# One hybrid decoder layer: half of the first FFN matrix by seven block products, the second matrix over eight banks, a longer gate queue and another first norm

## The chip, the core and the metric

The kernel runs on one core of one Trainium2 chip. The metric is the device time in microseconds of one execution. The profile shows one execution; its span is the time from the first to the last instruction.

## What is computed

One layer on 512 tokens of width 1024, all in float32: a norm, one wide projection, three causal attention mixers (sparse top-k, compressed and windowed, dilated), gates for each mixer, an output projection, and a gated FFN of hidden width 2816. Cut to what matters here:

```python
h = _rms(x, norm1_g)
(a_q, a_k, a_v, i_q, i_k, i_w, b_q, b_kv, b_g, c_qkv, mix_g) = _split_last(h @ w_in, IN_SIZES)
...                                    # three attentions give y_a, y_b, y_c of width 1024
g = sigmoid(mix_g).reshape(bsz, seq, 3, D_MODEL)
x = x + (g[:, :, 0] * y_a + g[:, :, 1] * y_b + g[:, :, 2] * y_c) @ w_out
h = _rms(x, norm2_g)
gate, up = split(h @ w_ffn_in, 2)      # each 512 x 2816
x = x + (silu(gate) * up) @ w_ffn_out
```

## The kernel before

**Matmuls in three passes.** Every large matrix product is done on pairs: a tensor is split into a high part in fp32r and a low part, the rest (`split`, lines 81 and 82: ScalarE casts, VectorE or GpSimd subtracts). `mm3` (lines 106 to 108) then issues three matmuls for each contraction block of 128: high by high, high by low, low by high. `weights` loads a block of a matrix by DMA on SP's queue (`raw`, five buffers, line 93) and splits it (`whi`, `wlo`, six buffers each, two contraction blocks of 256 columns in each); it is issued with high priority, so it runs as far ahead as buffers allow. The order of instructions on each engine is laid down ahead of the run by the framework, by priority and by the free buffers.

**The front.** Four tiles of 128 tokens are loaded on SP's queue. For each, `norm_sums` takes the squares of one half on ScalarE (line 162) and of the other on VectorE (line 164), `norm_T` adds the two sums (line 170), GpSimd makes the reciprocal root (lines 149 and 151), VectorE and ScalarE scale a half each (`hn`, lines 176 and 178), TensorE transposes eight blocks (line 111), VectorE multiplies the gain in (`gx`, line 188), and the result is split into `xh` and `xl`, one low part on GpSimd and one on VectorE. The first projection ("narrow", 220 columns, tokens stationary) follows, then all others, 256 weight columns at a time.

**Gates and merges.** For each of three branches and eight blocks of 128 output features, `gate` projects (24 matmuls of 512 columns, `pm<-xh,whi` and its two companions) and puts a tanh into a `tz` buffer (line 962, three buffers). `merge` projects the branch's heads (`pm<-oT`), combines the two (line 979) and writes to or reads from a DRAM tile `dz` (lines 973 and 984). A queue `due` keeps one gate ahead of each merge. The attention's steps are advanced between the halves of these projections (`tick`).

**Output projection and second norm.** `w_out` is taken in four groups of 256 columns, tokens stationary (`pf<-whi,zh`). In the last group each token tile is normalised, transposed and split into `xh2`, `xl2`.

**FFN.** The first matrix is taken in eleven chunks of 256 gate and 256 up columns. In a chunk the weights stand still and the hidden columns move: 2 (gate, up) x 2 column halves x 8 contraction blocks x 3 passes = 96 matmuls of 512 tokens. Chunk 0 is done in two token halves of 256, 192 matmuls, since the second half's norm comes later. After each half chunk ScalarE takes a tanh (line 1127), VectorE two gating operations (lines 1128 and 1129), and the result is split at once into `hh`, `hl`. The second matrix runs over 22 contraction blocks twice, once for each 512 output columns, into four PSUM banks at a time; tokens are stationary (`pf<-whi,hh`). At the end of each pass the last three blocks are done bank by bank, and each bank is added to the residual and written out (lines 1150 and 1151).

Of the kernel before, what the change touches and what calls it, by code (L numbers as in the profile page):

```python
# [67 lines left out]
def block_kernel(ctx: ExitStack, tc: tile.TileContext, x, norm1_g, norm2_g, w_in, qk_norm_g, cmp_pos, cmp_w,  # L68
# [60 lines left out]
    ip = ipx.enter_context(tc.tile_pool(name="init", bufs=1))  # L129
    with tc.high_priority():  # L130
# [4 lines left out]
    gT = ip.tile([128, KC], F32, name="gT")  # L135
    nc.scalar.dma_start(gT, norm1_g[0].rearrange("(k p) -> p k", p=128))
# [30 lines left out]
    def norm_T(xt, t, ss, n, g, xh, xl, pst, tmp, lo):  # L167

        s1 = ty.tile([128, 16], F32, name="nss", tag="ss")
        nc.vector.tensor_reduce(out=s1[:, 0:1], in_=ss[:, 0:n], op=ALU.add, axis=AX.X)  # L170
        r = rstd(s1, 1, 1.0 / D)
        hn = tmp.tile([128, D], F32, name="hn", tag="hn", bufs=2)
        for q in range(2):
            hs = slice(q * 512, q * 512 + 512)
            if q == 0:
# [4 lines left out]
        for q in range(2):  # L180
# [4 lines left out]
            if g is not None:  # L185
                g3 = g[:, 4 * q:4 * q + 4].unsqueeze(2).to_broadcast([128, 4, 128])
                gx = tmp.tile([128, 4, 128], F32, name="gx", tag="gx", bufs=2)
# [20 lines left out]
    xl = xp.tile([128, KC, S], F32R, name="xl", tag="xl")  # L208
    for t in range(NT):
# [42 lines left out]
    def proj_tm(segs, evac, then=None):  # L252
        width = sum(n for _, n in segs)
        wk = weights(w_in, segs, list(range(KC)), pool=PP)
# [29 lines left out]
    def tmt(name):  # L284
        return ap_.tile([128, NT, 256], F32, name=name, tag="tm", bufs=3)
# [80 lines left out]
    def narrow():  # L366
# [25 lines left out]
        proj_tm([(C_AKV, 128), (C_IK, 68), (C_BG, 24)], evac, then=then)  # L392
# [157 lines left out]
    def causal_probs(q, i, k, tab, topk, gate):  # L550
# [4 lines left out]
        if topk is not None:  # L555
            tm_ = ab.tile([128, S], F32, name="tabm", tag="tabm", bufs=2)
# [394 lines left out]
    def gate(bi, f):  # L951
# [9 lines left out]
        tz = ap_.tile([128, 2, S], F32, name="tz", tag="tm", bufs=3)  # L961
# [96 lines left out]
    norms = []  # L1058
    for c in range(0, D, 256):
# [11 lines left out]
        for t in range(NT):  # L1071
# [10 lines left out]
            if last:  # L1082
                norms.append(norm_T(xg[t], t, ss2[t], 4, None, xh2, xl2,
                                    lambda: m2_tile().rearrange("p (k c) -> p k c", c=128), np_,
                                    (nc.vector, nc.vector)))
                next(norms[t])

# [18 lines left out]
    for j in range(2):  # L1106
        ffn_in(pus[j], wu, j, lo_t, 4, KC)
        ffn_in(pus[j], wu, j, hi_t)
    nx.close()
    zx.close()  # L1110

    hp_ = ctx.enter_context(tc.tile_pool(name="hid", bufs=1, reuse_waits="tile"))
    hh_, hl_ = [], []
    for c in range(0, DFF, 256):
        if c:
            wg = weights(w_fi, [(c, 256)], list(range(KC)))
            pgs = [m2_tile() for _ in range(2)]
            for j in range(2):
                ffn_in(pgs[j], wg, j)
            wu = weights(w_fi, [(DFF + c, 256)], list(range(KC)))  # L1120
            pus = [m2_tile() for _ in range(2)]
        for j in range(2):
            pu = pus[j]
            if c:
                ffn_in(pu, wu, j)
            th = hp_.tile([128, S], F32, name="fth", tag="fth", bufs=2)
            nc.scalar.activation(th, pgs[j], AF.Tanh, scale=0.5)
            nc.vector.scalar_tensor_tensor(out=th, in0=th, scalar=1.0, in1=pgs[j], op0=ALU.add, op1=ALU.mult)
            nc.vector.scalar_tensor_tensor(out=th, in0=th, scalar=0.5, in1=pu, op0=ALU.mult, op1=ALU.mult)
            f = c // 128 + j  # L1130
            a = hp_.tile([128, S], F32R, name=f"hh{f}")
            b = hp_.tile([128, S], F32R, name=f"hl{f}")
            split(a, b, th)
            hh_.append(a)
            hl_.append(b)
# [35 lines left out]
```

## Time and profile before

| | us |
|---|---|
| median of 3 runs | 993.58 |
| lowest, highest | 992.93, 999.28 |
| the profiled execution | 991.78 |
| its span | 990.0 |

In the span TensorE is busy 971.0 us, VectorE 564.9, ScalarE 436.5 and GpSimd 174.0. Busy time of TensorE is modelled, and overlapping matmuls hide their own latency in it; so the number of matmuls in a stretch says more than the busy share. The stretches: front to about 29 us, projections and attention to about 573, output projection to about 616, second norm and chunk 0 to 647, ten chunks to 863, second matrix to 986, output to 990.

### The profile page before, as it was taken

What the parts mean: (1) busy time and instruction counts of PE and PEld (TensorE: products, weight loads), DVE (VectorE), ACT (ScalarE), POOL (GpSimd) and SP (SyncE); (2) the same over time, 40 slices, a digit from 0 to 9 for tenths busy, and PEclk for the clock granted to TensorE, in tenths of its full rate; (3) what the DMA queues carried; (4) which work ended last, traced back from release to release, by engine and by line L of the source; (5) the groups of instructions that cost most, each with busy time, mean ns of one, the idle gap of its engine ahead of it and who ended that gap; (6) DMA issues with size and microseconds to landing.
All of it is one profiled execution on the core that took longest, in us unless ns stands there. A gap on an engine that the chain in (4) does not pass through costs nothing.

```text
span 990.0 us, 16079 instructions
## 1 busy us (share of the span) xinstructions
PE 971.0 (98%) x5887; PEld 823.7 (83%) x5887; DVE 564.9 (57%) x1277; ACT 436.5 (44%) x956; POOL 174.0 (18%) x156
## 2 busy tenths in 40 slices
PE   6999999999999899999999999999999999999998
PEld 5889999899887577777778899988888888888886
DVE  6699999766665666574764645454344344422321
ACT  5544555756565655564534434443333233322220
POOL 3234565543100221131110312000000000000000
PEclk9999999999999999999999999999999999999999
DMA  8541344433332244367613452233333333322421
GB/s 210 123 128 44 86 119 128 120 116 110 104 96 66 79 129 121 118 167 195 187 57 89 140 201 86 86 101 110 88 88 108 104 85 96 110 93 96 139 75 42
DMA packets 119264, 109.91 MB, mean 111 GB/s; under 512 B 19931, under 2 KB 105234, under 8 KB 119186
## 3 DMA queue, kind: packets, MB, share of 16 engines
q1 hardware_dynamic: 116994, 107.85, 37.6%
q10 hardware_dynamic: 2192, 1.05, 0.4%
q8 instruction: 46, 0.75, 0.3%
q14 instruction: 32, 0.26, 0.1%
HBM read 96.66 MB, written 12.21 MB: 110 GB/s over the span
## 4 chain that ended last, share of the span: by engine, by line
PE 93%; DMA 3%; DVE 2%; ACT 1%; issue 1%; SPq 1%; POOL 0%; DVEq 0%; ACTq 0%; POOLq 0%
PE pf L107 14%; PE pf L108 14%; PE pf L106 14%; PE pm L107 13%; PE pm L106 13%; PE pm L108 13%; PE tr L111 4%; PE ovb L541 2%; PE lg L364 2%; PE lg L363 2%; PE ova L541 1%; DMA c_in<-dC 1%; PE lg L849 1%; DMA raw<-in_w_in 1%; DMA raw<-in_w_branch_a 1%
## 5 line engine op out<-in xcount | busy, mean ns | idle before, releaser
L82 DVE TENSOR_TENSOR wlo<-raw,whi 128x512 fp32r<-128x512 f32 (+1 forms) x243 | 182.4, 756 | 146.1 <-ACT whi L81 145.1
L81 ACT CAST whi<-raw 128x512 fp32r<-128x512 f32 (+1 forms) x288 | 176.9, 619 | 175.0 <-PE pf L108 80.8
L107 PE MATMUL pm<-wlo,xh 128*128 128x256 f32 (+1 forms) x512 | 145.5, 287 | 0.3 <-DVE wlo L82 0.3
L106 PE MATMUL pm<-whi,xh 128*128 128x256 f32 (+1 forms) x512 | 145.1, 288 | 0.6 <-ACT bgt L374 0.6
L108 PE MATMUL pm<-whi,xl 128*128 128x256 f32 (+1 forms) x512 | 144.8, 285 | 0.5 <-POOL xl L82 0.5
L107 PE MATMUL pf<-xl,whi 128*128 128x512 f32 (+1 forms) x384 | 142.6, 372 | 0.1
L106 PE MATMUL pf<-xh,whi 128*128 128x512 f32 (+1 forms) x384 | 142.5, 372 | 0.0
L108 PE MATMUL pf<-xh,wlo 128*128 128x512 f32 (+1 forms) x384 | 142.0, 371 | 0.0
L107 PEld LDWEIGHTS pm<-wlo,xh 128*128 128x128 f32 x512 | 98.1, 192 | 1.9 <-issue 0.8
L108 PEld LDWEIGHTS pm<-whi,xl 128*128 128x128 f32 x512 | 98.2, 192 | 1.4 <-POOL xl L82 0.8
L106 PEld LDWEIGHTS pm<-whi,xh 128*128 128x128 f32 x512 | 97.7, 193 | 1.2 <-ACT bgt L374 0.8
L108 PE MATMUL pm<-xh,wlo 128*128 128x512 f32 x224 | 88.8, 396 | 0.0
L106 PE MATMUL pm<-xh,whi 128*128 128x512 f32 x224 | 88.7, 396 | 0.0
L107 PE MATMUL pm<-xl,whi 128*128 128x512 f32 x224 | 88.1, 393 | 0.0
L107 PEld LDWEIGHTS pf<-xl,whi 128*128 128x128 f32 x384 | 72.3, 188 | 12.5 <-DVE xl L82 0.3
L106 PEld LDWEIGHTS pf<-xh,whi 128*128 128x128 f32 x384 | 72.2, 188 | 12.5
L108 PEld LDWEIGHTS pf<-xh,wlo 128*128 128x128 f32 x384 | 72.2, 188 | 12.6
L82 POOL TENSOR_TENSOR wlo<-raw,whi 128x512 fp32r<-128x512 f32 x45 | 62.2, 1404 | 111.6 <-ACT whi L81 100.8
L106 PE MATMUL pf<-whi,hh 128*128 128x512 f32 x176 | 69.4, 395 | 0.0
L108 PE MATMUL pf<-whi,hl 128*128 128x512 f32 x176 | 69.4, 395 | 0.0
L107 PE MATMUL pf<-wlo,hh 128*128 128x512 f32 x176 | 69.4, 395 | 0.0
L562 ACT ACTIVATE p<-p,m 128x128 f32<-128x128 f32 (+3 forms) x96 | 53.8, 561 | 27.2 <-DVE m L547 26.0
(312 smaller groups left out, 1691.0 us busy)
## 6 DMA issues: line engine op xcount, KB each, us to landing
raw<-in_w_in SPq DMA_DIRECT2D x92, 256.0 KB, 3.1
raw<-in_w_ffn_in SPq DMA_DIRECT2D x88, 256.0 KB, 2.9
raw<-in_w_ffn_out SPq DMA_DIRECT2D x44, 256.0 KB, 2.8
raw<-in_w_in SPq DMA_DIRECT2D x52, 128.0 KB, 2.6
x<-in_x SPq DMA_DIRECT2D x8, 512.0 KB, 6.0
tab<-dvec SPq DMA_DIRECT2D x16, 256.0 KB, 3.3
dz<-tz SPq DMA_DIRECT2D x16, 256.0 KB, 2.5
tz<-dz SPq DMA_DIRECT2D x16, 256.0 KB, 3.3
```

Of the source, the lines that this page charges most:

```text
L81: nc.scalar.copy(dst_hi, src)
L82: (eng or nc.vector).tensor_tensor(out=dst_lo, in0=src, in1=dst_hi.bitcast(F32), op=ALU.subtract)
L106: nc.tensor.matmul(ps, ah, bh, start=(j == 0), stop=False)
L107: nc.tensor.matmul(ps, ah, bl, start=False, stop=False)
L108: nc.tensor.matmul(ps, al, bh, start=False, stop=(j == n - 1))
L111: nc.tensor.transpose(dst, src, ident[0:src.shape[0], 0:src.shape[0]])
L363: nc.tensor.matmul(lg, qs, k[:, 0, 0:w], start=True, stop=False)
L364: return nc.tensor.matmul(lg, qs, k[:, 1, 0:w], start=False, stop=stop)
L541: mm = nc.tensor.matmul(ov[64 * j:64 * j + 64, 128 * b:S], v(b), pts[j][:, 4 * b:3 * b + NT, :], start=first and b == 0, stop=last and b = ...
L562: nc.scalar.activation(p[:, 0:w], p[:, 0:w], AF.Exp, bias=m[:, 0:1], scale=-1.0, accum_out=m[:, 1:2])
L849: nc.tensor.matmul(lg[32 * r:32 * r + 32, c:c + n], ld["q", g][hp, 128 * i + 32 * r:128 * i + 32 * r + 32], ld["k", g][hp, 128 * r:128 * r ...
```

## The change

**First FFN matrix.** Chunks 256, 768, 1280, 1792 and 2304 are computed by Winograd's form of Strassen's product. The blocks are gate or up columns by lower or upper half of the contraction (`a11`, `a21`, `a12`, `a22`), and lower or upper half of the contraction by first or second 256 tokens. Seven products of block sums take the place of eight block products. The weight sums `s1` to `s4` are made by VectorE in each chunk (8 operations of 512 elements) before the splits; the token differences `t1` to `t4` once, from an unsplit copy `xf` of the second norm that ScalarE takes out of PSUM. Each product is evicted by one or two VectorE additions into `ev` buffers. The next product chunk's loads and its first three sums stand in the plain chunk before it.

**Second matrix.** One loop over the 22 blocks fills all eight PSUM banks. The gated values stay unsplit in `hid` and are split block by block in this loop.

**Gates.** `due` holds two gates ahead; the `tm`/`tz` buffers are four. The masked table of the sparse attention shares the three `work` buffers.

**First norm.** The gain is spread over 128 partitions by two matmuls and multiplied in together with the scaling, on VectorE, before the transposes; squares of a tile are summed in one ScalarE operation; both low parts are made by VectorE. The narrow projection's weights are asked for after the second token tile.

```diff
+    g_row = ip.tile([1, D], F32, name="g_row")
+    nc.scalar.dma_start(g_row, norm1_g[0:1, :])
...
             xts.append(xt)
+            if t == 1:
+                w_narrow = weights(w_in, NARROW, list(range(KC)))
...
+            if g is not None:
+                nc.vector.scalar_tensor_tensor(out=hn[:, hs], in0=xt[:, hs], scalar=r[:, 0:1], in1=g[q], op0=ALU.mult,
+                                               op1=ALU.mult)
...
-                nc.vector.tensor_tensor(out=gx, in0=ps, in1=g3, op=ALU.mult)
-                ps = gx
             split(xh[:, 4 * q:4 * q + 4, ts], xl[:, 4 * q:4 * q + 4, ts], ps, eng=lo[q])
+            if xf is not None:
+                nc.scalar.copy(xf[:, 4 * q:4 * q + 4, ts], ps)
...
+    for q in range(2):
+        nc.tensor.matmul(gps[q], one, g_row[:, 512 * q:512 * q + 512], start=True, stop=True)
...
-        norm_sums(ss, xts[t], ip)
-        for _ in norm_T(xts[t], t, ss, 2, gT, xh, xl, tr_tile, ip, (nc.gpsimd, nc.vector)):
+        norm_sums(ss, xts[t], ip, n=1)
+        for _ in norm_T(xts[t], t, ss, 1, gps, xh, xl, tr_tile, ip, (nc.vector, nc.vector)):
...
-        tz = ap_.tile([128, 2, S], F32, name="tz", tag="tm", bufs=3)
+        tz = ap_.tile([128, 2, S], F32, name="tz", tag="tm", bufs=4)
...
-            if len(due) > 1:
+            if len(due) > 2:
...
+    for name, out_, p, q in (("t1", f11, f12, f11), ("t3", f12, f22, f12), ("t2", f22, f22, f11), ("t4", f21, f21, f22)):
+        th_, tl_ = (tp.tile([128, HK, S // 2], F32R, name=f"x{name}{v}") for v in "hl")
+        nc.vector.tensor_tensor(out=out_, in0=p, in1=q, op=ALU.subtract)
+        split(th_, tl_, out_)
+        xb[name] = (th_, tl_)
...
+    def fi_operands(c):
+        fr = {}
+        with tc.high_priority():
+            for r, (n, k) in enumerate((("a11", 0), ("a21", 0), ("a22", HK), ("a12", HK))):
+                for h in range(2):
+                    t_ = ep.tile([128, 2, 256], F32, name="fraw", tag="fraw", bufs=12)
...
+        def sums():
+            add("s1", None, "a21", "a22", ALU.add)
+            add("s2", None, "s1", "a11", ALU.subtract)
+            add("s3", "a21", "a11", "a21", ALU.subtract)
+        def get(n):
+            with tc.high_priority():
+                if n == "s4":
+                    add("s4", "s2", "a12", "s2", ALU.subtract)
...
+                    split(hi, lo, fr[n, h])
...
+        if c % 512 == 0:
...
+            if c + 256 < DFF:
+                sums, get = fi_operands(c + 256)
+            for j in range(2):
+                ffn_in(pus[j], wu, j)
+                if c + 256 < DFF and j == 0:
+                    sums()
+                swiglu(hid[c // 256][:, j, :], pgs[j], pus[j])
+            continue
...
+        for a, b in (("a11", "b11"), ("s2", "t2"), ("a12", "b21"), ("s3", "t3"), ("s1", "t1"), ("a22", "t4"), ("s4", "b22")):
+            w, (bh, bl) = get(a), xb[b]
+            ps = m2_tile()
+            for j in range(2):
+                cs = slice(128 * j, 128 * j + 128)
+                mm3(ps[:, 256 * j:256 * j + 256], [((w[k][0][:, cs], w[k][1][:, cs]), (bh[:, k, :], bl[:, k, :]))
+                                                   for k in range(HK)])
...
+    for k in range(NF):
+        for c in range(2):
+            wk[k, c] = weights(w_fo, [(512 * c, 512)], [k], per=1)[k]
+        hk[k] = [hs_.tile([128, S], F32R, name=f"hs{v}", tag=f"hs{v}", bufs=4) for v in "hl"]
+        split(*hk[k], hid[k // 2][:, k % 2, :])
+        if k < NF - LAST:
+            for c in range(2):
+                for t in range(NT):
+                    fo(k, c, t)
```

## Rows read from the trace of the kernel before

**Rows 1.** The page: busy time by engine, and the chain that ended last

```profile
PE 971.0 (98%) x5887; PEld 823.7 (83%) x5887; DVE 564.9 (57%) x1277; ACT 436.5 (44%) x956; POOL 174.0 (18%) x156
PE 93%; DMA 3%; DVE 2%; ACT 1%; issue 1%; SPq 1%; POOL 0%; DVEq 0%; ACTq 0%; POOLq 0%
```

**Rows 2.** Stages: us, busy (x instructions) PE PEld DVE ACT POOL, clock, DMA share, GB/s

```profile
0.00:18.60 18.60, 9.55 (x41) 8.65 (x42) 11.90 (x29) 11.79 (x23) 7.95 (x17) 1.00 0.84 212
...
320.00:332.60 12.60, 10.27 (x69) 7.15 (x67) 8.51 (x30) 10.07 (x26) 0.67 (x1) 1.00 0.41 105
332.60:336.10 3.50, 3.39 (x10) 1.24 (x12) 1.16 (x3) 0.55 (x3) 0.00 (x0) 0.51 0.00 0
336.10:345.00 8.90, 8.04 (x41) 4.57 (x37) 6.78 (x24) 5.36 (x18) 5.01 (x5) 1.00 0.10 32
...
573.00:616.00 43.00, 43.00 (x361) 43.00 (x360) 19.69 (x38) 16.40 (x45) 10.95 (x16) 1.00 0.44 147
616.00:628.40 12.40, 12.35 (x106) 12.14 (x105) 8.60 (x19) 8.35 (x18) 2.19 (x4) 1.00 0.28 86
628.40:646.70 18.30, 18.30 (x152) 18.12 (x151) 7.66 (x12) 6.76 (x12) 0.00 (x0) 1.00 0.19 58
646.70:863.40 216.70, 216.70 (x958) 179.43 (x957) 94.55 (x142) 72.21 (x121) 0.00 (x0) 1.00 0.35 99
863.40:986.30 122.90, 122.89 (x529) 99.28 (x527) 33.41 (x56) 24.82 (x40) 0.00 (x0) 1.00 0.28 92
986.30:990.00 3.70, 0.00 (x0) 0.00 (x0) 0.75 (x2) 0.00 (x0) 0.00 (x0) 1.00 0.21 73
```

**Rows 3.** VectorE's groups by line, 668.4 to 863: busy, mean ns | idle before

```profile
L82 DVE TENSOR_TENSOR wlo<-raw,whi 128x512 fp32r<-128x512 f32 x72 | 49.7, 691 | 33.1 <-ACT whi L81 33.1
L1128 DVE SCALAR_TENSOR_TENSOR fth<-fth,pf 128x512 f32<-128x512 f32 x18 | 12.3, 684 | 36.5 <-ACT fth L1127 36.5
```

**Rows 4.** ScalarE's casts of the second norm, group by line, 616 to 630

```profile
L81 ACT CAST xh<-pf 128x512 fp32r<-128x512 f32 x8 | 4.3, 592 | 3.1 <-PE pf L111 3.0
```

**Rows 5.** One line's instructions, VectorE on 1024 elements: duration ns min/median/max

```profile
L299 DVE TENSOR_TENSOR cqk_tm<-cqk_tm,rst x6: 1212/1225/1226, 161.3 to 229.1; 128x1024 f32<-128x1024 f32 x6
```

**Rows 6.** ScalarE's timeline of the gates' tanh; then a stage, gate matmuls alone

```profile
307.00 0.60 ACT L962 ACTIVATE tz<-pm 128x512 f32<-128x512 f32 x1 [0.86 <-PE pm L108]
347.72 0.60 ACT L962 ACTIVATE tz<-pm 128x512 f32<-128x512 f32 x1 [0.88 <-DMA dz<-tz]
...
320.80:348.00 27.20, 0.00 (x0) 0.94 0.30 86
```

**Rows 7.** TensorE's waits, 320 to 345: us in total, times, longest

```profile
PE tr L111 <- ACT pT L530: 1.9, 3, 0.7
```

**Rows 8.** Timelines of SP's queue and TensorE in the front: start, us, instructions

```profile
3.66 0.62 SPq L133 DMA_DIRECT2D x<-in_x  x1
5.59 6.27 SPq L93 DMA_DIRECT2D raw<-in_w_in  x10
...
29.39 0.40 PE L106 MATMUL pm<-xh,whi 128*128 128x512 f32 x1
```

**Rows 9.** TensorE's waits, 0 to 40

```profile
PE tr L111 <- DVE hn L176: 8.3, 2, 6.8
...
PE pm L108 <- POOL xl L82: 0.5, 1, 0.5
```

**Rows 10.** VectorE's and GpSimd's groups, 0 to 20: busy, mean ns | idle before

```profile
L188 DVE TENSOR_TENSOR gx<-tr,gT 128x512 f32<-128x512 f32 x5 | 3.4, 681 | 0.0
L164 DVE CUSTOM_DVE_ANT_0 nsq<-x 128x512 f32<-128x512 f32 x4 | 2.8, 690 | 4.0 <-DMA x<-in_x 4.0
L176 DVE TENSOR_SCALAR hn<-x,rst 128x512 f32<-128x512 f32 x4 | 1.9, 480 | 1.0 <-POOL rst L151 1.0
L170 DVE TENSOR_REDUCE nss<-nss 128x1 f32<-128x2 f32 x4 | 0.6, 152 | 0.3
...
L82 POOL TENSOR_TENSOR xl<-gx,xh 128x512 fp32r<-128x512 f32 x2 | 2.8, 1422 | 1.5 <-ACT xh L81 1.3
```

More of the change, by code (lines that the diff above doesn't have):

```diff
@@ L129, in block_kernel @@
     ip = ipx.enter_context(tc.tile_pool(name="init", bufs=1))
+    NARROW = [(C_AKV, 128), (C_IK, 68), (C_BG, 24)]
+    g_row = ip.tile([1, D], F32, name="g_row")
+    nc.scalar.dma_start(g_row, norm1_g[0:1, :])
+    one = ip.tile([1, 128], F32, name="one")
+    nc.vector.memset(one, 1.0)
     with tc.high_priority():
@@ L249, in rev, with proj_tm @@
         return bass.AP(tensor=tab.tensor, offset=tab.offset + hi - 1, ap=[list(tab.ap[0]), [-1, hi - lo]])
-    def proj_tm(segs, evac, then=None):
+    def proj_tm(segs, evac, then=None, wk=None):
         width = sum(n for _, n in segs)
-        wk = weights(w_in, segs, list(range(KC)), pool=PP)
+        wk = wk or weights(w_in, segs, list(range(KC)), pool=PP)
         for t in range(NT):
@@ L1108, in block_kernel @@
         ffn_in(pus[j], wu, j, hi_t)
+    HK = KC // 2
+    tp = ctx.enter_context(tc.tile_pool(name="tsum", bufs=1, side="right", reuse_waits="tile"))
+    fx = ExitStack()
+    ep = fx.enter_context(tc.tile_pool(name="ev", bufs=1, side="right", reuse_waits="tile"))
+    xb = {"b11": (xh2[:, 0:HK, lo_t], xl2[:, 0:HK, lo_t]), "b21": (xh2[:, HK:KC, lo_t], xl2[:, HK:KC, lo_t]),
+          "b22": (xh2[:, HK:KC, hi_t], xl2[:, HK:KC, hi_t])}
+    f11, f12, f21, f22 = (xf[:, k, t] for k in (slice(0, HK), slice(HK, KC)) for t in (lo_t, hi_t))
@@ new lines, in swiglu @@
+    def swiglu(dst, g, u):
+        th = ep.tile([128, 512], F32, name="fth", tag="fth", bufs=2)
+        nc.scalar.activation(th, g, AF.Tanh, scale=0.5)
+        nc.vector.scalar_tensor_tensor(out=th, in0=th, scalar=1.0, in1=g, op0=ALU.add, op1=ALU.mult)
+        if len(dst.shape) == 3:
+            th, u = (v.rearrange("p (j t) -> p j t", j=2) for v in (th, u))
+        nc.vector.scalar_tensor_tensor(out=dst, in0=th, scalar=0.5, in1=u, op0=ALU.mult, op1=ALU.mult)
+    for j in range(2):
+        swiglu(hid[0][:, j, :], pgs[j], pus[j])
@@ L1116, in block_kernel @@
+    sums, get = fi_operands(256)
+    sums()
+    for c in range(256, DFF, 256):
+        if c % 512 == 0:
             wg = weights(w_fi, [(c, 256)], list(range(KC)))
-            pgs = [m2_tile() for _ in range(2)]
+            wu = weights(w_fi, [(DFF + c, 256)], list(range(KC)))
+            pgs, pus = ([m2_tile() for _ in range(2)] for _ in range(2))
             for j in range(2):
                 ffn_in(pgs[j], wg, j)
-            wu = weights(w_fi, [(DFF + c, 256)], list(range(KC)))
-            pus = [m2_tile() for _ in range(2)]
@@ L1122, in block_kernel @@
[L1122 to L1135, printed above, removed]
@@ L1136, in block_kernel @@
-    for c in range(0, D, 512):
-        pss = [m2_tile() for _ in range(NT)]
-        wk = {}
-        for k in range(NF):
-            wk.update(weights(w_fo, [(c, 512)], [k], per=1))
-            for t in range(NT if k < NF - LAST else 0):
-                ts = slice(t * 128, (t + 1) * 128)
-                mm3(pss[t], [((hh_[k][:, ts], hl_[k][:, ts]), wk[k])], k, NF)
+            if c + 256 < DFF:
[3 more added lines that the diff above has]
+                if c + 256 < DFF and j == 0:
+                    sums()
+                swiglu(hid[c // 256][:, j, :], pgs[j], pus[j])
@@ new lines, in block_kernel, with fo @@
+    fx.close()
+    hs_ = ctx.enter_context(tc.tile_pool(name="hsp", bufs=1, reuse_waits="tile"))
+    pss = [[m2_tile() for _ in range(NT)] for _ in range(2)]
+    wk, hk = {}, {}
+    def fo(k, c, t):
+        ts = slice(t * 128, (t + 1) * 128)
+        mm3(pss[c][t], [((hk[k][0][:, ts], hk[k][1][:, ts]), wk[k, c])], k, NF)
+    for k in range(NF):
[7 more added lines that the diff above has]
+                    fo(k, c, t)
```

80 lines of the change are left out of this document (59 added, 21 removed).

## Prediction

> **What bounds the kernel now.** I read the page's head and chain first, then the stages, then who waits for whom. The head shows TensorE busy 98% of the span and the chain gives it 93% [rows 1]. Busy is not yet full use, so the stage table is read for matmuls per microsecond. Ten plain chunks of the first FFN matrix fill 646.7 to 863.4: 10 x 96 matmuls of 512 columns in 216.7 us, 225.7 ns each and 21.67 us a chunk, with no gap. VectorE is busy 94.55 us there, 44%, ScalarE 33%, the DMA engines 35% [rows 2]. The second matrix takes 528 matmuls in 122.9 us, 232.8 ns each, again gapless, and 3.7 us of output follow [rows 2]. So in the last 340 us only less TensorE work shortens anything. Elsewhere two stretches are not full. In the front TensorE is busy 9.55 of 18.6 us. From 320 to 345 it idles 3.3 us, and in 332.6 to 336.1 the granted clock is 0.51, its lower level, after the idle before it [rows 2].
>
> **The Winograd products.** Five of eleven chunks (256, 768, ..., 2304) change; chunk 0 and the five others keep 96 full-width matmuls. A product has two column halves of 4 contraction blocks with 3 passes: 24 matmuls of 256 columns, and seven are 168 in place of 96 of double width. The trace holds the price: chunk 0 runs the same operands (weights stationary, 256 hidden columns moving) in 628.4 to 646.7, 152 matmuls in 18.3 us, 120.4 ns [rows 2]. Thus 168 x 0.1204 = 20.23 us against 21.67: 1.44 us a chunk, **7.2 us for five**, not the eighth (13.5 us) that counting products suggests; two narrow matmuls cost 240.8 ns where a wide one costs 225.7. The output projection's 361 in 43.0 us (119.1 ns) give 8.3 us, the upper bound.
>
> The page "TensorE: Matmul & The Clock Gate" of the Trainium skill, section "Back-to-back issue gap", speaks against this: it gives a stream of load and matmul pairs about 81 ns at 128 columns and 131 ns at 512. By an estimate on the line between, 256 columns cost 98 ns, and 168 of them 16.4 us against 12.6 for 96 wide ones, a loss of 3.8 us a chunk. The trace's two rates do not agree with it [rows 2], and the sum goes by them.
>
> **Do VectorE and ScalarE keep up?** A 512-element split, sum or eviction takes VectorE 0.69 us (691 to 684 ns, by group) [rows 3]. A product chunk asks for 8 sums, 14 low parts, 7 additions out of PSUM and 4 gating operations: 33 x 0.69 = 22.8 us against 20.2 of TensorE, too much alone. But the first three sums (6 operations) are issued inside the plain chunk before, and the six buffers each for high and low parts let three products be split ahead. That leaves at most 27 x 0.69 = 18.6 us; the plain chunk holds 8 + 4 + 6 = 18, 12.4 us of 21.67. Over the pair 31 of 41.9 us, so VectorE hides, at 74%. Were that cover gone, each product chunk would cost up to 22.8 us. ScalarE has 14 casts, one copy and 2 tanh, about 17 x 0.62 = 10.5 us. Evictions may lag: eight banks hold seven products. I charge 0.5 us for all five chunks (bounds 0 and 5 x 2.6 = 13).
>
> **Preparing the products, once.** Eight copies of 512 columns from PSUM (the unsplit norm) join ScalarE, priced like its casts there, 592 ns: 4.7 us [rows 4], in a stretch where ScalarE is busy 8.35 of 12.4 us. Two or three stand ahead of the second token tile's casts, which TensorE waits for: **1.0 us** (0 to 2). Then four differences and four low parts of 1024 elements, 1.22 us each by the nearest such row [rows 5], make 9.8 us of VectorE, and six sums 4.1. VectorE is busy 7.66 of 18.3 us in chunk 0's stretch, so 21.6 us want 18.3. The first product needs none of the differences; the second is due 2.9 us later. **1.5 us** (0 to 4).
>
> **Second matrix over eight banks.** The same 528 matmuls with the same three-pass groups: zero. The 22 high and low splits of the gated values move here, 22 x 0.69 = 15.2 us on a VectorE busy 33.4 of 122.9 us. At the seam the new split buffers lie where the product buffers were; the last of these that I expect there is done a whole chunk earlier. If it were the last gating buffer instead, gating, cast and split (about 2 us) would stand in the open: bounds 0 and 2, taken as 0. The last bank still ends with nine matmuls, two additions and two writes, so the 3.7 us at the end stay.
>
> **Gates.** The ScalarE rows show the third tanh at 307 us and the fourth only at 347.72, released by a write-out of a gate buffer: three gate buffers were held by merges that lacked the branch's last heads, and from 320.8 to 348 not one gate matmul ran [rows 6]. Meanwhile TensorE waited on ScalarE's copies of the attention's transposes, 1.9 us [rows 7]. With four buffers and one more gate ahead of each merge, one gate (24 x 0.2257 = 5.4 us) can run in that hole. The hole shows 3.3 us idle and 3.5 us at half clock, worth 1.7: 5.0 in all. I take **4.5 us**. Bounds: 0, if PSUM or the gate's weights are missing, and 5.4.
>
> **First norm.** The first full-width projection starts at 29.39 us [rows 8]. Before that TensorE waits 8.3 us on the normalised rows and 0.5 on GpSimd's low part [rows 9]; VectorE is the one that lags, x's last tile having been asked for at 3.66 us [rows 8]. Per token tile VectorE loses a square sum (0.69), a reduction (0.15), a scaling (0.48) and two gain products (1.36), 2.68 us; it gains two scalings by two factors (at the same 0.69, PSUM operand as in gx) and the low part that GpSimd made in 1.42 us: 2.07 [rows 10]. Four times 0.6 is 2.4 us less VectorE, and the GpSimd step leaves the chain. The weights' 12 issues may now stand ahead of the last two token tiles; ten took SP 6.27 us [rows 8]. I take **3.0 us**; bounds: 2 lost, if those tiles wait for the issues, and 6 won, most of the idle time before 18.6. Broadcasting the gain costs two matmuls in time that is idle.
>
> **Sum.** Against the profiled run: 991.78 - 7.2 - 4.5 - 3.0 + 0.5 + 1.0 + 1.5 = 980.1. The median of the runs lies 1.8 higher: 993.58 - 11.7 = 981.9.
>
> **Rivals.** (A) The FFN gain comes alone: the front is set by loads and the hole by the attention's own chain, 981.9 + 7.5 = 989.4. For it: the hole's wait is between attention steps [rows 7]; against: it has no gate in it. (B) The side gains come, but VectorE's load around the products eats the FFN's 4.2 net: 986.1. For it: 18.6 of 20.2 us; against: a plain chunk of slack after each. (C) The slower end: splits do not run ahead, so that at every product chunk TensorE waits for six sums (4.1), a cast and split (1.3) and then goes at VectorE's 22.8 us: 28.2 us, 8.0 over, 40 for five, 981.9 - 0.5 + 40 = 1021.4. It decides from 2.4 us of wait a chunk (no gain) and from 4.4 is slower by over 1%. Against it: every plain chunk of before is split ahead without one wait. (D) Front and gates pay in full and nothing waits: 993.58 - 7.2 - 6 - 5.4 + 0.5 = 975.5. (E) Narrow matmuls lose their rate in the products: from 129 ns they gain nothing; at three quarters of a wide one, 169 ns, five chunks cost 34 more than before, 1023. The skill's section above would have it so; chunk 0's row excludes it nearly.
>
> **Chances.** Forecast 0.50 (own range 978 to 986), A 0.20, B 0.11, C 0.07, D 0.10, E 0.02. The range 975 to 991 takes in A, B and D. About 1% (983.6) is what a measurement of this kernel can tell from no change. Faster by more: D and most of the forecast, 0.54; within: the rest, A and B, 0.39; slower: C and E, 0.07.
>
> **What would show it.** Right: 168 matmuls of a product chunk in about 20.2 us without waits on low parts; second matrix 122.9 us; a gate's 24 matmuls inside the former hole; the first full-width projection near 26 us. Wrong: TensorE waiting for low parts or sums in the products, a lower granted clock, or a front that starts no earlier.

## The result and the profile after

The changed kernel takes 986.07 us (median, 984.40 to 986.10). The kernel before took 994.12 us on the same chip, so the ratio is 0.9917, with a 95% interval of 0.9892 to 0.9942: 8.05 us, or 0.8%, faster. The time lies in the forecast's range of 975 to 991, 4.2 us above its point of 981.9; the gain is just short of the 1% that the forecast held likeliest to be passed. The profiled execution took 984.40 us, with a span of 982.6 us; it is the fastest of the four, at a mean granted clock of 1.000, where the other three (986.05 to 986.10 us) had 0.996 to 0.998.

The page's head and its chain, after:

```profile
PE 964.2 (98%) x6251; PEld 831.8 (85%) x6251; DVE 634.2 (65%) x1379; ACT 462.9 (47%) x999; POOL 167.0 (17%) x152
PE 92%; DVE 3%; DMA 2%; ACT 1%; issue 1%; SPq 0%; POOL 0%; DVEq 0%; ACTq 0%
```

TensorE is still the bound, with 364 more matmuls in 6.8 us less busy time; VectorE went from 57% to 65% [rows 1]. The stages after, columns as in [rows 2]:

```profile
327.00:350.00 23.00, 18.81 (x105) 11.04 (x104) 16.22 (x49) 15.23 (x43) 7.13 (x8) 1.00 0.19 58
615.41:628.25 12.84, 12.41 (x106) 12.03 (x104) 8.77 (x19) 10.72 (x24) 2.22 (x4) 1.00 0.29 84
628.25:646.00 17.75, 17.44 (x144) 17.03 (x143) 15.80 (x19) 10.58 (x16) 0.00 (x0) 1.00 0.19 60
646.00:666.32 20.32, 20.32 (x173) 20.32 (x173) 19.25 (x32) 10.23 (x17) 0.00 (x0) 1.00 0.38 109
666.32:688.11 21.79, 21.79 (x99) 18.03 (x97) 13.92 (x21) 6.73 (x12) 0.00 (x0) 1.00 0.31 93
688.11:708.00 19.89, 19.89 (x170) 19.89 (x168) 15.14 (x24) 9.78 (x16) 0.00 (x0) 1.00 0.39 113
855.00:856.00 1.00, 0.01 (x1) 0.01 (x1) 0.97 (x2) 1.00 (x3) 0.00 (x0) 1.00 0.54 182
856.00:979.00 123.00, 122.95 (x528) 99.37 (x528) 44.97 (x76) 34.59 (x59) 0.00 (x0) 1.00 0.28 90
979.00:982.60 3.60, 0.00 (x0) 0.00 (x0) 0.74 (x2) 0.00 (x0) 0.00 (x0) 1.00 0.22 73
```

Read from the end. Output 3.6 us and second matrix 123.0 us are as before. One microsecond between the matrices (855 to 856) is new: TensorE did nothing there. A product chunk takes 19.9 us (the row of the first takes in the end of chunk 0), a plain one 21.8. By the rows the ten chunks fill 646 to 855, 209.0 us where there were 216.7 [rows 2], and the second norm and chunk 0 (615.41 to 646) take 30.6 us where they took 30.7. But 216.7 us is not all that the ten chunks took before. Four of their 960 wide matmuls had run ahead, inside chunk 0's stretch; the kernel before, TensorE (start, us, instruction), the first and the last of the four:

```profile
639.06 0.40 PE L106 MATMUL pf<-xh,whi 128*128 128x512 f32 x1
639.76 0.40 PE L107 MATMUL pf<-xl,whi 128*128 128x512 f32 x1
```

So 956 wide matmuls filled the 216.7 us, 226.7 ns each, and all 960 are worth 217.6 us. After, five product and five plain chunks of the lengths above are 208.4 us. The products thus bring about 9.2 us. The two stretches together got 7.8 us shorter (247.4 to 239.6), so the copies and token differences cost about 1.4 us in chunk 0's stretch. There TensorE idles 0.7 us in the two rows from 615.41 to 646.00, where it idled less than 0.1 before [rows 2]. In all the FFN accounts for 9.2 - 1.4 - 1.0 - 0.1 + 0.1 = 6.8 us. Everything ahead of it gave 0.7: the first matmul of the output projection's line starts at 572.2 us after and 572.9 us before (this view is one line's instructions: count, duration, first and last start).

```profile
L106 PE MATMUL pf<-whi,zh x128: 278/282/286, 572.2 to 619.6; 128*128 128x256 f32 x128
```

TensorE's waits after, from 0 to 60, 320 to 360 and 825 to 870 us: us in total, times, longest:

```profile
PE tr L111 <- DVE hn L182: 2.7, 2, 1.3
PE lg L217 <- DMA g_row<-in_norm_g: 2.2, 1, 2.2
...
PE tr L111 <- DVE p L573: 1.1, 3, 0.5
PE tr L111 <- ACT pT L539: 1.0, 2, 0.5
...
PE pf L106 <- ACT hsh L81: 1.0, 1, 1.0
```

The wait for the normalised rows fell from 8.3 to 2.7 us [rows 9], yet the end hardly came nearer. In the attention a wait on VectorE's scaling (p) stands where there was none [rows 7]. The last line is the new microsecond. The timelines after (start, us, instructions): ScalarE's tanh of the fourth gate, GpSimd and VectorE in the attention, TensorE in the front, and ScalarE at the end of the first matrix:

```profile
27.79 0.40 PE L106 MATMUL pm<-xh,whi 128*128 128x512 f32 x1
...
316.57 0.59 ACT L971 ACTIVATE tz<-pm 128x512 f32<-128x512 f32 x1
...
341.73 3.86 POOL L566 TENSOR_TENSOR tabm<-tab,topm 128x384 f32<-128x384 f32 x4 [4.98 <-DVE m L556]
343.73 2.00 DVE L573 TENSOR_SCALAR p<-p,m 128x256 f32<-128x256 f32 x2
...
854.80 0.62 ACT L81 CAST whi<-raw 128x512 fp32r<-128x512 f32 x1 [0.74 <-DVE wlo L82]
855.32 2.18 ACT L81 CAST hsh<-h 128x512 fp32r<-128x512 f32 x4
```

The fourth gate's tanh came at 316.57 instead of 347.72 us [rows 6]. Its products did not come earlier by as much: in the kernel before the last of them ran at 320.36 us, and only the tanh stood waiting for a buffer. What the fourth buffer set free is the fifth gate. In the stretch that had no gate matmul [rows 6] 21 of its 24 now run: 14 that read xh, and 7 that read xl, which a stage table of the xh tiles leaves out (us, TensorE busy and count, clock; first xh, then xl):

```profile
320.80:348.00 27.20, 4.18 (x14) 1.00 0.20 59
320.80:348.00 27.20, 2.65 (x7) 1.00 0.20 59
```

They all stand at its start. The first line is the last product of the fourth gate before, then come the first and the last product of the fifth gate after:

```profile
320.36 0.40 PE L108 MATMUL pm<-xh,wlo 128*128 128x512 f32 x1
...
319.80 0.39 PE L106 MATMUL pm<-xh,whi 128*128 128x512 f32 x1
326.30 0.40 PE L108 MATMUL pm<-xh,wlo 128*128 128x512 f32 x1
```

The seventh attention unit's products, which follow, start 4.4 us later than before (before, then after):

```profile
323.51 2.38 PE L541 MATMUL ovb<-pT,bv 128*64 128x512 f32 x16
327.88 2.37 PE L550 MATMUL ovb<-pT,bv 128*64 128x512 f32 x16
```

### The profile page after: what moved, and what is told of

Read it like the earlier page. It is cut to its first block, busy times and chain, and to the rows that moved or that the text cites. A ratio compares the mean times of both kernels' runs of the same rounds, so it can differ in the third digit from the quotient of the medians.

```text
span 982.6 us, 16956 instructions
## 1 busy us (share of the span) xinstructions
PE 964.2 (98%) x6251; PEld 831.8 (85%) x6251; DVE 634.2 (65%) x1379; ACT 462.9 (47%) x999; POOL 167.0 (17%) x152
## 4 chain that ended last, share of the span: by engine, by line
PE 92%; DVE 3%; DMA 2%; ACT 1%; issue 1%; SPq 0%; POOL 0%; DVEq 0%; ACTq 0%
PE pf L108 13%; PE pf L107 13%; PE pf L106 13%; PE pm L106 13%; PE pm L107 12%; PE pm L108 12%; PE tr L111 5%; PE ovb L550 2%; PE lg L372 2%; PE lg L373 2%; PE ova L550 1%; PE lg L858 1%; DVE wlo L82 1%; PE ovc L903 1%; DMA x<-in_x 1%
## 5 line engine op out<-in xcount | busy, mean ns | idle before, releaser
L81 ACT CAST whi<-raw 128x512 fp32r<-128x512 f32 (+1 forms) x248 | 152.2, 618 | 127.4 <-PE pf L108 43.2
L82 DVE TENSOR_TENSOR wlo<-raw,whi 128x512 fp32r<-128x512 f32 (+1 forms) x203 | 150.5, 747 | 83.6 <-ACT whi L81 79.1
L106 PE MATMUL pf<-xh,whi 128*128 128x256 f32 (+1 forms) x344 | 114.4, 333 | 0.1
L107 PE MATMUL pf<-xl,whi 128*128 128x256 f32 (+1 forms) x344 | 114.3, 333 | 0.0
L108 PE MATMUL pf<-xh,wlo 128*128 128x256 f32 (+1 forms) x344 | 114.0, 333 | 0.2 <-DVE wlo L82 0.2
L106 PEld LDWEIGHTS pf<-xh,whi 128*128 128x128 f32 x344 | 65.0, 189 | 6.6 <-ACT whi L81 0.3
L108 PEld LDWEIGHTS pf<-xh,wlo 128*128 128x128 f32 x344 | 64.9, 189 | 6.6 <-DVE wlo L82 0.4
L106 PE MATMUL pf<-whi,hsh 128*128 128x512 f32 x176 | 69.4, 395 | 1.0 <-ACT hsh L81 1.0
L107 PE MATMUL pf<-wlo,hsh 128*128 128x512 f32 x176 | 69.4, 395 | 0.0
L108 PE MATMUL pf<-whi,hsl 128*128 128x512 f32 x176 | 68.3, 395 | 0.0
```

What stands on the lines that cost most here:

```text
L81: nc.scalar.copy(dst_hi, src)
L82: (eng or nc.vector).tensor_tensor(out=dst_lo, in0=src, in1=dst_hi.bitcast(F32), op=ALU.subtract)
L106: nc.tensor.matmul(ps, ah, bh, start=(j == 0), stop=False)
L107: nc.tensor.matmul(ps, ah, bl, start=False, stop=False)
L108: nc.tensor.matmul(ps, al, bh, start=False, stop=(j == n - 1))
```

## The experiments

Times are medians, each set against the kernel before on the same chip. The changed kernel was measured twice, the second time as the fourth run, which turned out to be the same program.

| kernel | us | ratio, 95% interval |
|---|---|---|
| changed | 986.07 | 0.9917 (0.9892 to 0.9942) |
| 1 short queue of gates | 988.30 | 0.9941 (0.9921 to 0.9961) |
| 2 all chunks plain | 992.15 | 0.9983 (0.9972 to 0.9994) |
| 3 old first norm | 984.41 | 0.9901 (0.9884 to 0.9918) |
| 4 early split asked for (same program) | 984.69 | 0.9905 (0.9887 to 0.9923) |
| 5 old gates and tabm buffers | 986.28 | 0.9921 (0.9894 to 0.9947) |
| 6 ten product chunks | 978.35 | 0.9838 (0.9812 to 0.9865) |
| 7 the same, sums on GpSimd | 994.96 | 1.0007 (0.9992 to 1.0022) |
| 8 attention first | 1037.65 | 1.0433 (1.0402 to 1.0464) |
| 9 FFN part alone | 986.47 | 0.9919 (0.9893 to 0.9945) |
| 10 ten chunks, early split | 975.49 | 0.9807 (0.9778 to 0.9836) |
| 11 the same, weights in pairs | 975.34 | 0.9804 (0.9775 to 0.9832) |
| 12 as 10, old front | 975.96 | 0.9814 (0.9788 to 0.9841) |

**Is the gain the FFN's?** Run 2 makes all chunks plain again and keeps everything else.

```diff
-    sums, get = fi_operands(256)
-    sums()
-        if c % 512 == 0:
+        if True:
```

> The changed kernel with all eleven chunks plain; the token differences are still made, though nothing reads them. By the forecast's 1.44 us a chunk this run is 7.2 us slower than the changed kernel (986.1), 993.3; by the trace after (19.9 us a product chunk against 21.8) 9.5 us slower, 995.6. If VectorE's load around the products ate the gain it is within 3 us of 986.1.

Measured 992.15 us, 6.1 and 7.5 us above the changed kernel's two medians: 1.2 to 1.5 us a chunk, less than either sum expected. A part of the difference is the seam: with plain chunks TensorE does not wait there, so the products lose that 1.0 us again. The rest of the change, with the first norm, the gates and the eight banks, is worth 0.17% (0.06 to 0.28). Run 9 turns it round: the FFN part stays and the first norm, the gates and the tabm buffers are as before.

```diff
-            if len(due) > 2:
+            if len(due) > 1:
-            tm_ = ab.tile([128, S], F32, name="tabm", tag="work", bufs=3)
+            tm_ = ab.tile([128, S], F32, name="tabm", tag="tabm", bufs=2)
-        norm_sums(ss, xts[t], ip, n=1)
-        for _ in norm_T(xts[t], t, ss, 1, gps, xh, xl, tr_tile, ip, (nc.vector, nc.vector)):
+        norm_sums(ss, xts[t], ip)
+        for _ in norm_T(xts[t], t, ss, 2, gT, xh, xl, tr_tile, ip, (nc.gpsimd, nc.vector)):
```

> The FFN part of the change alone (five chunks from products, the second matrix over eight banks, the float copies and token differences that the products need), with the first norm, the queue of gates and the tabm buffers as before. If the whole gain is the FFN's, the ratio to the kernel before is that of the changed kernel, 0.990 to 0.992, 984.5 to 986.5 us. If the traces' shorter FFN stretch (247.3 to 240.6 us, 6.7 us) is all that it gives and the side parts give the rest, 987.4 us. If the side parts give what was forecast for them (7.5 us), 993.5 us less the surplus of the FFN, about 992 us.

Measured 986.47 us, ratio 0.9919 against 0.9917: the FFN alone gives a gain as large as the whole change. The intervals are 2.5 us wide to either side, so the 7.5 us forecast for the side parts are excluded, one or two are not. The traces agree with a small gain: with the changed front and a clock of 1.00 up to there, the output projection starts at 571.7 to 572.5 us (after, runs 2, 4, 6 and 11), with the old front at 572.9 (run 12).

**The first norm.** Run 3 puts the old one back (gain multiplied behind the transposes, square sums in two halves, one low part on GpSimd; the norm's lines of the diff above).

> The changed kernel with the first norm as before (gain behind the transposes, one low part on GpSimd, square sums halved, narrow weights after all token tiles). If all that the trace after shows at the first full-width projection (27.79 against 29.39 us) arrives at the end, this run is 1.6 us slower than 986.1, 987.7; by the forecast 3.0 slower, 989.1; if later stretches absorb the shift, no difference.

Measured 984.41 us, not slower than the changed kernel. The traces say where the shorter front goes. The first full-width projection starts at 27.79 us after and at 29.39 before [rows 8], 1.6 us earlier. But that one trace is at the end of what the new norm gives. Run 4, the same program, starts it 0.8 us later than the changed kernel's own trace:

```profile
28.61 0.41 PE L106 MATMUL pm<-xh,whi 128*128 128x512 f32 x1
```

Over all traces with this projection behind the new norm, run 8 aside, it starts at 27.79 to 29.17 us, and with the old norm at 29.11 to 29.42 (before, runs 3, 9 and 12). From 60 to 165 us VectorE is the busy one, 102.57 of 105 us. The first product of an attention unit starts at 192.1 us after and at 192.9 before; in run 6, also with the new norm, it starts at 193.1. After:

```profile
L550 PE MATMUL ovb<-pT,bv x80: 272/432/644, 192.1 to 286.4; 128*64 128x512 f32 x20, 128*64 128x384 f32 x20, 128*64 128x256 f32 x20, 128*64 128x128 f32 x20
```

What is left there is below what the traces and the times tell apart.

**The gates.** Run 1 makes the queue one gate long again and leaves tabm in the shared buffers; run 5 also gives tabm its own two buffers back.

```diff
-            if len(due) > 2:
+            if len(due) > 1:
```

> The changed kernel with the gate part alone undone: one gate ahead of a merge and three gate buffers, as before. The changed kernel took 986.1 us. If the extra gate fills the hole near 330 us, as forecast, this run is 4.5 us slower, about 990.6. If the extra gate only runs ahead of the hole, in a stretch that has no slack, and the hole moves along, this run stays within 1 us of 986.1, and its trace shows the hole some 4 to 5 us earlier and about as long.

```diff
-            tm_ = ab.tile([128, S], F32, name="tabm", tag="work", bufs=3)
+            tm_ = ab.tile([128, S], F32, name="tabm", tag="tabm", bufs=2)
```

> The changed kernel with the whole gate stage as it was before: the queue of gates is again one long, as in the run with the short queue (988.3 us), and the masked tables (tabm) have their own two buffers again instead of sharing the three of work. If the shared buffers are what made the short queue slow (four tabm additions of GpSimd in a row, and VectorE's scaling beside them at 1.0 us each instead of 0.44), the time falls back by about the 1.9 us that the stretch from the second ovb to the merges grew, or more, to 984.5 to 986.5 us, at or below the changed kernel. If the length of the queue alone decides, it stays at 988.3 us, and the four us between it and the changed kernel are what one more gate in the queue is worth.

Run 1 came out at 988.30 us, 2.2 to 3.6 above the changed kernel, run 5 at 986.28, level with it. That the shared buffers cost some 2 us and the longer queue gives them back is not shown. The intervals of the two runs overlap, and the executions differ in their granted clock: the one of run 1 at 1.000 took 984.95 us, the one of run 5 at 1.000 took 985.38. The rows show what the buffers do in one place, not what that is worth at the end. Run 1, GpSimd's masked tables, VectorE's scaling and its first merge:

```profile
339.81 3.86 POOL L566 TENSOR_TENSOR tabm<-tab,topm 128x384 f32<-128x384 f32 x4 [7.75 <-DVE m L556]
341.81 2.01 DVE L573 TENSOR_SCALAR p<-p,m 128x256 f32<-128x256 f32 x2
347.00 1.27 DVE L988 SCALAR_TENSOR_TENSOR tz<-tz,pm 128x512 f32<-128x512 f32 x2
```

Run 5, the same lines:

```profile
338.08 1.80 POOL L566 TENSOR_TENSOR tabm<-tab,topm 128x384 f32<-128x384 f32 x2 [7.70 <-DVE m L556]
339.20 0.84 DVE L573 TENSOR_SCALAR p<-p,m 128x256 f32<-128x256 f32 x1
340.97 0.95 DVE L573 TENSOR_SCALAR p<-p,m 128x256 f32<-128x256 f32 x1
343.50 0.68 DVE L988 SCALAR_TENSOR_TENSOR tz<-tz,pm 128x512 f32<-128x512 f32 x1
```

With three buffers GpSimd makes four tables in a row, and both scalings of 256 elements lie beside them, 2.0 us for the pair. With two it pauses, but the pair still takes 1.8. The first merge comes 7.2 us after the first of these tables in run 1 and 5.4 in run 5. In the changed kernel the rows of the tables and the scalings are the same as in run 1. TensorE's wait on VectorE's scaling (p, 1.1 us) stands in run 1 too and not in run 5, so it comes with the shared buffers and not with the longer queue.

Run 8 was to put each step of the attention ahead of the gates near it.

```diff
-                next(g)
+                with tc.high_priority(400):
+                    next(g)
```

> The changed kernel in which each step of the attention is put in the order ahead of the gates' products that stand near it, so that gates only fill what the attention leaves open. If the hole between 327 and 350 us is the attention's own chain of latencies and gates are merely used up too early before it, the gates now lie in the hole: its 4.2 us of idle TensorE go, 981 us. If the waits only move to where no gate is left, as with the longer queue, the time stays within 1.5 us of the changed kernel (984.7 to 986.1 us). If the attention's instructions in front of everything else hold up the projections that feed them, it is slower than 988 us.

Measured 1037.65 us, and the trace shows that the edit did not do what it was for: the first attention unit came at 283.1 us instead of 192.1. So it tells nothing about the hole, only that disturbing this order can cost 50 us. Run 8, the unit's line, as above:

```profile
L551 PE MATMUL ovb<-pT,bv x16: 272/432/643, 283.1 to 285.2; 128*64 128x512 f32 x4, 128*64 128x384 f32 x4, 128*64 128x256 f32 x4, 128*64 128x128 f32 x4
```

**What bounds a product chunk?** Run 6 makes all ten later chunks from products, with the next chunk's sums inside the present one.

```diff
-        if c % 512 == 0:
+        if False:
+        nxt = fi_operands(c + 256) if c + 256 < DFF else None
             elif a == "s1":
                 add_ps("c22", "u2", ps)
+                if nxt:
+                    nxt[0]()
```

> All ten later chunks of the first FFN matrix from seven products, the sums still on VectorE. If TensorE sets the length of a chunk as in the measured product chunk (19.9 us against 21.8 us for a plain one), five more chunks bring 5 x 1.9 = 9.5 us: 976 us. If VectorE becomes the bound, a chunk takes what its instructions take: 14 casts' differences, 7 additions of products, 4 steps of the gating and 8 sums of blocks, 33 x 0.685 us = 22.6 us; ten of them are 226 us against the 208.5 us of five and five, so 17.5 us slower than the changed kernel, about 1003 us, slower than the kernel before.

Measured 978.35 us. The expectation that VectorE makes it slower, 33 x 0.685 us a chunk, fell. Run 6's stages:

```profile
640.00:840.00 200.00, 200.00 (x1682) 199.64 (x1681) 194.48 (x320) 99.95 (x166) 0.00 (x0) 1.00 0.31 92
840.00:850.00 10.00, 7.63 (x59) 7.21 (x58) 9.02 (x15) 5.33 (x10) 0.00 (x0) 1.00 0.49 150
```

Run 6, TensorE's waits from 640 to 860 us, all there are:

```profile
PE pf L106 <- ACT hsh L81: 2.4, 1, 2.4
```

Run 6, VectorE's timeline (start, us, instruction):

```profile
711.79 0.69 DVE L82 TENSOR_TENSOR wlo<-fraw,whi 128x512 fp32r<-128x512 f32 x1
712.39 0.69 DVE L1168 TENSOR_TENSOR fraw<-fraw 128x512 f32<-128x512 f32 x1
712.99 0.69 DVE L1143 SCALAR_TENSOR_TENSOR fth<-fth,eu 128x512 f32<-128x512 f32 x1
```

TensorE never waits in the chunks: 1682 matmuls in 200 us, 118.9 ns each. VectorE is 97% busy and keeps up, because its instructions start 0.60 us apart though each lasts 0.69. At that spacing 33 of them take 19.8 us, a little under the chunk's 20. Its duration is not its price in a stream. (Seven of the 33 are additions of products; the first product is taken out of PSUM by a copy on ScalarE.)

Run 7 moves the sums s1 to s4 to GpSimd.

```diff
-                nc.vector.tensor_tensor(out=fr[n, h], in0=fr[p, h], in1=fr[q, h], op=op)
+                nc.gpsimd.tensor_tensor(out=fr[n, h], in0=fr[p, h], in1=fr[q, h], op=op)
```

> As the run with ten product chunks, but the sums s1 to s4 on GpSimd. VectorE then has 25 x 0.685 us = 17.1 us in a chunk, less than TensorE's 19.9 us. If GpSimd's work lies freely beside VectorE's, the gain is the whole 9.5 us: 976 us. If the two hinder each other as beside the tabm additions (the scaling of 128x256 on VectorE took 1.0 us instead of 0.44, the addition on GpSimd 0.9 to 1.9 us), the eight sums of a chunk take 8 us and more of GpSimd, and VectorE's instructions beside them twice their time: 17.1 us + 8 x 0.685 us = 22.6 us or more for a chunk, 1003 us or more.

Measured 994.96 us, 16.6 above run 6. Run 7's groups by line, 640 to 860 us (busy, mean ns | idle before):

```profile
L82 DVE TENSOR_TENSOR wlo<-fraw,whi 128x512 fp32r<-128x512 f32 x80 | 85.3, 1069 | 0.0
L1210 DVE TENSOR_TENSOR eu<-eu,pf 128x512 f32<-128x512 f32 x38 | 25.8, 679 | 0.0
L1143 DVE SCALAR_TENSOR_TENSOR fth<-fth,eu 128x512 f32<-128x512 f32 x9 | 15.0, 1662 | 0.1
...
L1143 DVE SCALAR_TENSOR_TENSOR fth<-fth,ea 128x512 f32<-128x512 f32 x10 | 6.8, 682 | 0.1
...
L1168 POOL TENSOR_TENSOR fsum<-fraw 128x512 f32<-128x512 f32 x18 | 39.5, 2193 | 72.6 <-DMA fraw<-in_w_ffn_in 39.4 <-DVE eu L1210 33.2
```

Run 7, TensorE's waits in the same stretch:

```profile
PE pf L108 <- DVE wlo L82: 12.9, 16, 1.3
```

Run 7's stage from 700 to 740 us, and one of GpSimd's additions in it:

```profile
700.00:740.00 40.00, 37.73 (x314) 37.12 (x313) 40.00 (x48) 18.40 (x32) 24.32 (x14) 1.00 0.33 94
...
711.48 3.00 POOL L1168 TENSOR_TENSOR fsum<-fraw 128x512 f32<-128x512 f32 x1 [6.52 <-DMA fraw<-in_w_ffn_in]
```

VectorE has eight instructions fewer a chunk and is later all the same: it is busy all of these 40 us with 48 instructions. A low part from two SBUF tiles takes 1069 ns on average instead of 692, a gating step (fth<-fth,eu) 1662 instead of 691. An addition with one input in PSUM keeps its 679 ns. The Trainium skill's page "SBUF — State Buffer", section "Who interferes with whom", says that a VectorE instruction with two SBUF inputs contends with GpSimd's reads and one with a single SBUF input, outside certain faster modes, does not; these three rows agree. The fourth VectorE row, also a gating step from two SBUF tiles, keeps 682 ns: in this stretch it runs at 705.43 and 727.64 us, while GpSimd is idle. And it is not always VectorE that pays: at 712.03 a gating step (h<-fth,eu) took its old 0.68 us beside the GpSimd addition shown last, and that one took 3.00 us, where the next five took 1.72 to 1.74.

**The seam.** Run 4 only asked for an early order of the first splits of the hidden values.

```diff
-        split(*hk[k], hid[k // 2][:, k % 2, :])
+        with tc.high_priority():
+            split(*hk[k], hid[k // 2][:, k % 2, :])
```

> The changed kernel with the split of each gated block in the second matrix issued with high priority. TensorE waits 1.0 us at the seam for ScalarE's cast of the first gated block. If that cast is late only because it is queued behind weight casts, this run shows no wait there and is 1.0 us faster, 985.1; if the cast waits for memory of the product buffers, the wait stays and the time with it.

The instruction order of every engine came out unchanged, so this run is a second look at the changed kernel: 984.69 us, 1.4 us from the first one. Run 10 gives the first two splits tiles that are free a chunk earlier.

```diff
+        if k < 2:
+            hk[k] = [v[:, 2 * k:2 * k + 2, :].rearrange("p j t -> p (j t)") for v in xb["t2"]]
+            with tc.high_priority():
+                split(*hk[k], hid[0][:, k, :])
```

> As the run with ten product chunks (978.35 us), but the first two casts of the hidden values (hsh, hsl) go into the tiles of one token difference that the last chunk no longer reads, so they need not wait until the FFN's pool is closed. If TensorE's 2.4 us at the seam are that wait, they go: 976 us. If the casts stand behind the weights' casts in ScalarE's order anyway, or VectorE, 19.9 us busy of 20 us in a chunk, is late with the difference, the time stays within 0.7 us of 978.35 us.

Measured 975.49 us, 2.9 below run 6, and the wait of 2.4 us is gone from the trace; TensorE is busy through (run 10's stages, also 870 to 960 us of the second matrix):

```profile
840.00:850.00 10.00, 10.00 (x73) 9.41 (x73) 8.74 (x15) 4.26 (x7) 0.00 (x0) 1.00 0.38 112
870.00:960.00 90.00, 90.00 (x389) 73.00 (x388) 32.40 (x52) 26.21 (x45) 0.00 (x0) 1.00 0.25 82
```

So the splits were held by the buffers, which become free only when the FFN's pool is closed, and not by ScalarE's queue alone. Run 10 also asks for an early order, but run 4 shows that this alone changes nothing.

**The second matrix in pairs.** Run 11 orders six matmuls to a bank instead of three.

```diff
+                for t in range(NT):
+                    for k in ks:
+                        fo(k, c, t)
```

> As the run before it, and in the second FFN matrix two rows of weights are taken together, so that six matmuls in a row, not three, go into one PSUM bank. In the traces a 128x512 matmul follows the one before it after 232.4 to 233.3 ns where the bank changes every three, and after 226.9 ns where 24 in a row stay in one bank. If the change of bank costs the 6 ns (3 x 6 = 18 ns a change), half of the changes save 88 x 18 = 1.6 us or less: about 974.5 us. If the difference comes from something else (the operands, the clock), the time and the spacing stay.

Nothing: 975.34 us. Run 11's stage, to be read beside run 10's row of the same stretch:

```profile
870.00:960.00 90.00, 90.00 (x387) 72.40 (x386) 31.55 (x52) 25.42 (x45) 0.00 (x0) 1.00 0.26 85
```

387 matmuls in 90 us where run 10 had 389. With half the changes of bank in the program's order, a wide matmul here (231 to 233 ns) is as much slower than in a plain chunk (227 ns) as with all of them, so the change of bank is not what does it, unless the order on the engine was another: the trace does not name the banks. What does is open.

**The best version without the side parts.** Run 12 is run 10 behind the old first norm, gates and tabm buffers; its edits are those of runs 6, 9 and 10.

> The FFN with ten product chunks and the early first cast (975.5 us with the changed front), and in front of it the first norm, the queue of gates and the tabm buffers of the kernel before. If the side parts are worth nothing, as the run with the FFN part alone says (ratio 0.9919 against 0.9917 for the whole change), the ratio to the kernel before stays at 0.981, 975 to 976.5 us. If they are worth what was forecast for them (7.5 us), it is 983 us; if the two us by which the traces of the changed kernel reach the output projection earlier are theirs, 977.5 us.

Measured 975.96 us, ratio 0.9814 against 0.9807. The side parts are worth nothing that these times tell from zero. Runs 10 to 12 beat both kernels: 1.9% below the kernel before, 1.1% below the changed one by the ratios.

## Why the prediction was right or wrong

The time was in the range, but the way there was rival A's, the FFN gain alone, with an FFN worth more than forecast. That it came 4.2 us from the point and not 6.8 is luck: the side parts brought 6.8 us too little and the FFN 2.6 too much, and the two errors have opposite signs. The figure itself, 986.07, is rival B's (986.1), whose story is the reverse of what the traces show. Step by step, forecast against the two profiled runs, whose spans differ by 7.4 us:

| step | forecast | shown |
|---|---|---|
| ten chunks, five as products | -7.2 | about -9.2 (217.6 to 208.4) |
| VectorE inside them | +0.5 | 0, TensorE never waits there |
| copies and token differences | +2.5 | about +1.4 |
| seam | 0, bounds 0 and 2 | +1.0 |
| second matrix and output | 0 | 0 |
| gates and first norm | -7.5 | -0.7; not told from 0 by the times of runs 9 and 12 |

**The products: right in mechanism, better in size.** 168 narrow matmuls took 19.9 us against the 20.23 worked out from chunk 0, a plain chunk 21.8 against 21.67. So a product chunk saves 1.9 us and not 1.44. The smaller part of the error is a reading: 216.7 us were divided by 960 matmuls where 956 had run, and the 152 matmuls from which chunk 0's price was taken hold the other four. The larger part is that narrow matmuls go at 118 ns in the products and went at 120 in chunk 0. Rival E falls: 118.9 ns each over 200 us. By the estimate from the Trainium skill's page "TensorE: Matmul & The Clock Gate", section "Back-to-back issue gap", it would have been 98 ns, with wide ones at 131; this trace agrees with neither, and the run decides.

**VectorE's price: wrong step.** The prediction priced its stream at 0.69 us an instruction, the duration, and so had 22.8 us for a product chunk's 33 operations and 21.6 for chunk 0's stretch. In run 6 such operations start 0.60 us apart. By that ratio the 21.6 become some 19, and the prepared operands were nearly always ready: VectorE is busy 15.80 of 17.75 us there, and TensorE idles 0.3. So of the 3 us charged for VectorE and ScalarE about 1.4 came true, all of it ahead of the chunks, and with the right price all ten chunks fit. Rivals B and C, both built on a late VectorE, fall; run 7 shows what their mechanism looks like when it does happen.

**The seam: the bound was right, the value not.** The prediction named the case, the splits' buffers freed by the last gating, and took 0. It cost 1.0 us, and 2.4 with ten chunks; run 10 removed it.

**The gates: the step that failed.** One more gate did run, so the held buffer was rightly read from [rows 6], and 21 of the fifth gate's 24 products even lie in the stretch from 320.8 to 348. What failed is the next step, that its 5.4 us would replace idle time. They stand at 319.80 to 326.7 us, ahead of the time in which TensorE idles, and TensorE still idled 4.2 us, now in 327 to 350, where it had idled 3.3. A gate's product waits for nothing but a buffer, so it runs as soon as it stands in line, and the attention's steps behind it come later: the seventh unit's products by 4.4 us. The rows show this for one gate; run 8, which was to hold the gates back, did not do so. Shown is also that the times with the gates as before (run 5, run 9, run 12) are not told from those with the longer queue. A part of it was new cost: the buffers of tabm were given up for the fourth gate buffer, a wait on VectorE's scaling came of it, and the prediction put no price on that line of the diff.

**The first norm: half the start at best, none at the end.** The wait on the normalised rows shrank as forecast, and a new one came ahead of it, on the load of the gain's row (g_row, 2.2 us). The first full-width projection gained 1.6 of 3.0 us in the trace after, 0.8 in run 4; at the first attention unit nothing sure is left, and run 3 shows no loss with the old norm. The step to find fault with is adding an earlier start to the sum as if it travelled to the end. Between lies a stretch, 60 to 165 us, in which VectorE is busy almost throughout; that this is what eats the start is not tested.

The half-clock stretch of before (0.51 in 332.6 to 336.1 [rows 2]) comes and goes whatever the gates: with the old queue run 5 has one there (clock 0.89 over 325 to 340), and runs 9 and 12 have none in 320 to 350 (1.00); with the longer queue runs 3 and 10 have one (0.57 and 0.60 over 336 to 340) and the changed kernel none. It is not shown to belong to the order of the gates, and the 1.7 us it was worth should not have stood in the forecast as something the longer queue wins. Nor did it cost that at the end. Run 12 has the front of before without it. Its eighth tanh comes at 387.05 us where it came at 388.68, but its output projection starts at 572.9, as before:

```profile
L106 PE MATMUL pf<-whi,zh x128: 278/282/286, 572.9 to 620.4; 128*128 128x256 f32 x128
```

From 360 to 575 us TensorE waits 1.7 us more there, on a load (c_in, 2.7 us for 1.8) and on VectorE (oT, 0.8). So in this pair of traces an earlier end of the attention's hole, too, is eaten by what follows.

## What to carry to other kernels

Price a stream of instructions by the distance from start to start in a full stretch, not by the duration of one; here 0.60 against 0.69 us decided whether five or ten chunks could be products. Filler work shortens a hole only if it is held back until the hole comes: see in the order what stands ahead of it, and what must give up its buffers for it. An earlier start is a gain only if nothing between there and the end eats it: before it goes into a sum, look for what the stretches behind it wait for.

## What the runs showed of the hardware

- VectorE's 128x512 operations follow each other at 0.60 us while each record lasts 0.69 (run 6).
- GpSimd beside VectorE: low parts from 692 to 1069 ns on average, one gating step from 691 to 1662, an addition with a PSUM input unchanged at 679; the gating step that runs while GpSimd is idle keeps 682. GpSimd's own addition of 128x512 took 1.5 to 2.2 us on average (run 7). The scaling of 256 elements took 0.84 and 0.95 us beside two tabm additions (run 5) and 1.0 beside four (run 1), where 16 scalings of this size in another part of the attention took 0.44 on average (kernel before).
- A stretch of 3.5 us at the lower clock, in a part where TensorE waits on the attention's steps, left the start of the output projection where it was in one pair of traces: 572.9 us with it (before) and without it (run 12).
- The wide matmuls of the second matrix run at 231 to 233 ns, whether three or six in a row are ordered to a bank, against 227 in the plain chunks; this is not explained.
